# Four projection steps in a round: output products of a linear-attention mixer moved from the stage after it into its rounds

## Chip, cores, metric

The program runs on one core of one Trainium2 chip. The metric is the device time of one execution in microseconds; the time before is 2855.52 us, the median of three runs (2850.24 to 2856.83). Engines are named as the profile names them: PE (TensorE), DVE (VectorE), ACT (ScalarE), POOL (GpSimd) and SP, whose queue issues most DMAs.

## The reference, cut to what matters

One step of a two-layer trunk of width 1024 over 1072 columns (16 meta tokens, 32 frames of a running stream, 1024 of a new one). In layer 0 two mixers share one projection in and one out; mixer A is sliding-window attention, mixer B gated linear attention with four heads:

```python
def gla_chunk(S, q, k, v, g):
    b = jnp.cumsum(g, axis=2)
    decay = jnp.exp(jnp.where(causal[:, :, None], b[:, :, :, None, :] - b[:, :, None, :, :], -jnp.inf))
    att = jnp.einsum('bhtd,bhsd,bhtsd->bhts', q, k, decay)
    o = jnp.einsum('bhtd,bhdv->bhtv', q * jnp.exp(b), S) + jnp.einsum('bhts,bhsv->bhtv', att, v)
    bl = b[:, :, -1:, :]
    S_new = jnp.exp(bl[:, :, 0, :, None]) * S + jnp.einsum('bhsd,bhsv->bhdv', k * jnp.exp(bl - b), v)
    return S_new, o
...
gb = jax.nn.log_sigmoid((glr @ w_gate + b_gate)) / GATE_TAU           # the gate of mixer B
ob = rmsnorm(ob, onorm).reshape(B_, L, H_B * DV_B) * jax.nn.silu(rb)
x = x + jnp.concatenate([oa, ob], axis=-1) @ w_out                    # ab_output, both mixers
x = x + mlp(rmsnorm(x, norm_mlp[l]), w_up[l], w_down[l])              # each layer
```

Layer 1 (another mixer and its MLP) is not touched.

## The kernel before, in words

Activations lie transposed: 128 features on the partitions, tokens in the free dimension. `xT` (128 x 8 x 1072) is the residual. Every product in 32-bit accuracy is made of three matmuls: each operand is split into a high part (ACT, a cast, L64) and a low part (DVE, the difference, L66), and `mm3` adds high x high, high x low and low x high (L75, L76, L77).

`mixer_b` works through the nine token tiles (48 and eight of 128) in twelve rounds, t = -2 to 9, as a pipeline: a round makes the output of tile t-1 (`gla_output`: masked scores times values, states, norm and gate into `gl_sq`), the features of t+2 (transposes), the scores of t in six levels (`gla_levels`, two halves of three; `copy_predicated` on DVE writes them into `gl_att`, L662), the decays of t+1 (`gla_decays`: sums of gates by matmul, exponentials `gl_X` on ACT, and with them `gl_Q` and a new `gl_X` on DVE and POOL), the gate of t+2 (`gla_gate`), the inputs of t+1, the states of t (`gla_states`, `gl_S`, L685), and the transposes of the finished tile t-1 (`gla_finish`, L722) with the split into `mixb`. The gate log sigmoid(x) is min(x, 0) - ln(1 + exp(-|x|)): ACT makes the second part, DVE (L566) joins the two and reads x from PSUM.

The output projection fills PE between these parts. Its steps come from the generator `out_ab`, one at each `next(fill)`. A step is one product (`add_product`): 12 matmuls (four blocks of 128 features by three) into one PSUM bank, which DVE then adds into `xT` (L833). `ob` is one of eight blocks of 128 output features and has a weight tile of its own (`weights`: a DMA of 256 KB on SP's queue, then the split into `op_h` and `op_l`). Mixer A's part comes first, 8 x 3 = 24 products over `CHUNKS` (304, 384 and 384 columns); then mixer B's for the first of four `QUARTERS` (268 columns each) and ob 0 to 3, four products after the last round. The rounds take two steps each.

What is left of mixer B's part, 28 products, follows in `body`, here called the norm stage: quarter by quarter, `product(q, ob)`, its weights kept in `wb`. After a quarter, `spill(q)` stores it to DRAM (one DMA, on SP's queue), and `mlp_norm(q, between)` makes the sums of squares (`nm_acc`), PE's mean, the scaling of `xT` in place (L873) and the MLP's operands `ho_B`; `between` holds three products of the next quarter, issued between the squares and the mean. The MLP's first two products need quarters 0 and 1, its third (`ho_T`) the differences of all four.

PE's order in `mixer_b` is the order of the code (`manual_schedule`). The other engines' order, and PE's outside, is set by the framework's scheduler. All banks of one product, of transposes, decays, gate and states come in turn from one pool of four (`bank`): a request takes the buffer of the fourth request before it and waits for that buffer's last reader. The masked scores and the output have another pool of two (`b2`).

Of the kernel before, what the change touches and what calls it, by code (L numbers as in the profile page):

```python
# [12 lines left out]
AF = mybir.ActivationFunctionType  # L13
ALU = mybir.AluOpType
# [6 lines left out]
KB = 8  # L21
# [7 lines left out]
QUARTERS = [[(268 * q, 268 * q + 268) for q in range(4)], [(16 + 264 * q, 280 + 264 * q) for q in range(4)]]  # L29
# [22 lines left out]
class Core:  # L52
# [501 lines left out]
    def gla_gate(self, t, d, sb):  # L554
        nc = self.nc
        r0, m = TILES[t]
        px = self.bank()
        nc.tensor.matmul(px[:m, :256], self.aug[t % 2][:, :m], self.wg, start=True, stop=True)

        e = sb.tile([P, 256], F32, name="gl_e", bufs=1)  # L560
        g = sb.tile([P, 256], F32, name="gl_g", bufs=1)
        gh, gl = d["g"] = [sb.tile([P, 256], F32R, name=f"gl_g{x}") for x in "hl"]
        nc.scalar.activation(e[:m], px[:m, :256], AF.Abs)
        nc.scalar.activation(e[:m], e[:m], AF.Exp, scale=-1.0)
        nc.scalar.activation(e[:m], e[:m], AF.Ln, bias=1.0)
        nc.vector.scalar_tensor_tensor(g[:m], px[:m, :256], 0.0, e[:m], op0=ALU.min, op1=ALU.subtract)  # L566
        self.hi_lo(g[:m], gh[:m], gl[:m])


# [181 lines left out]
                pass  # L751


    ahead = 4

    def out_ab(self, sb, xs):
        w = self.i["w_out_ab"][0]
        for ob in range(KB):
            for k in (0, 1) if ob == 0 else (ob + 1,) if ob + 1 < KB else ():

                self.nc.vector.tensor_copy(self.xT[0:1, k, 0:1], self.z0[0:1, 0:1])
                self.nc.sync.dma_start(self.xT[:, k], xs[:, k])
            wt = self.weights(sb, w, 0, 4, P * ob, P, "op", 2)
            for c in CHUNKS:
                self.add_product(wt, self.mixa, 0, c, ob, c[0])
                yield
        for ob in range(self.ahead):
            wt = self.weights(sb, w, 4, 4, P * ob, P, "op", 2)
            self.add_product(wt, self.mixb, 0, QUARTERS[0][0], ob, 0)
            yield  # L770


    def mixer_b(self, fill):
        tc, nc = self.tc, self.nc
        with ExitStack() as st:
            self.b2 = st.enter_context(tc.tile_pool(name="myb2", bufs=2, space=PSUM, reuse_waits="tile"))
            sb = st.enter_context(tc.tile_pool(name="my2", bufs=2, reuse_waits="tile"))
            st.enter_context(tc.manual_schedule(engines={mybir.EngineType.PE}))
            n = len(TILES)
            d = {}  # L780

            def stage(f, t, *a):
                if 0 <= t < n:
                    f(t, d[t], *a)

            def load(t, what):
                if 0 <= t < n:
                    self.gla_load(t, d.setdefault(t, {}), sb, what)

            self.glq = [sb.tile([P, 2, 6, 2, 64], F32, name=f"gl_Q{x}", bufs=1) for x in range(2)]  # L790
            for q in self.glq:
                nc.gpsimd.memset(q, 0.0)
            load(0, "z")
            self.z0 = d[0]["z"]
            for t in range(-2, n + 1):
                load(t + 3, "z")
                load(t + 2, "r")
                load(t + 1, "v")
                stage(self.gla_output, t - 1, sb)
                stage(self.gla_features, t + 2, sb)  # L800
                next(fill)
                stage(self.gla_levels, t, (0, 1, 2))
                stage(self.gla_decays, t + 1, sb)
                stage(self.gla_gate, t + 2, sb)
                stage(self.gla_inputs, t + 1, sb)
                stage(self.gla_levels, t, (3, 4, 5))
                stage(self.gla_finish, t - 1)
                stage(self.gla_states, t, sb)
                next(fill)

            for _ in fill:
                pass

# [809 lines left out]
def body(tc, i, o):  # L1623
    C = Core(tc, i, o)
    nc = tc.nc
    with ExitStack() as st:
# [18 lines left out]
        def right(name):  # L1645
            return tc.tile_pool(name=name, bufs=1, side="right", reuse_waits="tile")

        C.bank = banks(st.enter_context(tc.tile_pool(name="bank", bufs=4, space=PSUM, reuse_waits="tile")))
        with right("h0") as h0:
            C.hp = [h0] * 3  # L1650
            mixes = ExitStack()
            with right("kv") as c1, right("w0") as wsb:
                fill = C.project_a(xs, wsb, c1)
# [11 lines left out]
        with mixes:  # L1665
            mix = mixes.enter_context(tc.tile_pool(name="mixb", bufs=1, reuse_waits="tile"))
            C.mixb = [mix.tile([P, 4, T], F32R, name=f"mixb_{x}") for x in "hl"]
            xp = st.enter_context(right("x1"))
            C.xT = xp.tile([P, KB, T], F32, name="xT")
            op = mixes.enter_context(tc.tile_pool(name="op", bufs=2, reuse_waits="tile"))  # L1670
            C.mixer_b(C.out_ab(op, xs))
            hpool = ExitStack()
            C.nm = mixes.enter_context(tc.tile_pool(name="nm1", bufs=1, reuse_waits="tile"))
            wb = {}
            with tc.tile_pool(name="op2", bufs=6, reuse_waits="tile") as op2:
                def weights(ob):
                    if ob not in wb:
                        raw = op.tile([P, 4, P], F32, name="op_", bufs=2)
                        sb = op if ob in (2, 3) else op2
                        wb[ob] = [sb.tile([P, 4, P], F32R, name=f"op_{x}", bufs=2 if sb is op else 6) for x in "hl"]  # L1680
                        nc.sync.dma_start(raw, i["w_out_ab"][0].rearrange("(k p) n -> p k n", p=P)[:, 4:8, P * ob:P * ob + P])
                        C.hi_lo(raw, *wb[ob])
                    return wb[ob]
                def product(q, ob):
                    c = QUARTERS[0][q]
                    C.add_product(weights(ob), C.mixb, 0, c, ob, c[0])

                C.mlp_begin(0)
                steps = [[partial(product, q, ob) for ob in range(0 if q else C.ahead, KB)] for q in range(4)]
                for q in range(4):  # L1690
                    while steps[q]:
                        steps[q].pop(0)()
                    C.spill(q)
                    if q < 3:
                        C.mlp_norm(q, [steps[q + 1].pop(0) for _ in range(3)])

        hpool, nms = ExitStack(), ExitStack()
        nxt, sq, ys = [], {}, {}
# [142 lines left out]
```

## Time and profile before

| | us |
|---|---|
| median of three runs | 2855.52 (2850.24 to 2856.83) |
| profiled execution, its own time | 2860.78 |
| its span | 2859.0 |
| mean granted clock of PE | 0.962 of full speed |
| mixer B (360 to 557.4) | 197.4 |
| norm stage (557.4 to 650.8, from the split of the last transposes to PE's start on `ho_T`) | 93.4 |

Times in the profile count from the span's start. In a table by stage each engine has its busy time and, in brackets, its instructions; behind them stand the clock that the throttle granted PE (1.00 is full speed), the share of the DMA engines' time and the data rate. A timeline row holds start, duration, engine, line, operation, output and inputs, shapes and count; in square brackets stands how long the engine had been idle and for whom. A row of waits holds total, number and longest.

### The profile page before, as it was taken

How to read it: one execution, taken by the hardware profiler on the slowest of the kernel's cores; microseconds unless marked ns; L12 is line 12 of the kernel's file. 1: busy time of each engine (PE TensorE's matmuls, PEld its weight loads, DVE VectorE, ACT ScalarE, POOL GpSimd, SP SyncE). 2: the span in 40 equal slices, each digit the busy share in tenths (PEclk: the TensorE clock that was granted, in tenths of full speed). 3: DMA queues.
4: the chain of work that ended last, by engine and by line, in shares of the span. 5: the costliest groups of instructions: out<-in, count | busy, mean ns of one | idle time of the engine just before them, and what ended most of it. 6: DMA issues, size and time to landing. Idle time of an engine off the chain costs nothing. (4 is left out here: it accounts for less than half of the span.)

```text
span 2859.0 us, 49166 instructions
## 1 busy us (share of the span) xinstructions
PE 2642.7 (92%) x18377; PEld 2452.5 (86%) x18391; DVE 1891.1 (66%) x3846; ACT 1265.2 (44%) x2820; POOL 631.0 (22%) x693
## 2 busy tenths in 40 slices
PE   5899988878999999999999978999977999999998
PEld 5888966768999999999789856788767999989998
DVE  5934376687676677578643556778788676677553
ACT  4435454243333335445333346666653333435342
POOL 3423354200000210003110244555521000111000
PEclk9999988999999999999999979999988999999999
DMA  6343241132544577544465374344322434486643
GB/s 192 101 133 103 73 140 43 31 112 92 163 131 153 208 231 218 171 136 121 119 197 168 116 175 128 88 100 103 77 85 71 157 135 156 173 265 204 198 141 102
DMA packets 355926, 393.77 MB, mean 138 GB/s; under 512 B 41503, under 2 KB 292088, under 8 KB 353640
## 3 DMA queue, kind: packets, MB, share of 16 engines
q1 hardware_dynamic: 338728, 305.50, 37.6%
q0 software_dynamic: 16960, 85.13, 8.2%
q8 instruction: 145, 2.38, 0.4%
q14 instruction: 93, 0.76, 0.1%
HBM read 263.94 MB, written 125.48 MB: 136 GB/s over the span
## 5 line engine op out<-in xcount | busy, mean ns | idle before, releaser
L75 PE MATMUL bank<-pj_wh,h 128*128 128x384 f32 (+3 forms) x832 | 298.0, 360 | 9.5 <-ACT pj_wh L64 7.0
L77 PE MATMUL bank<-pj_wh,h 128*128 128x384 f32 (+3 forms) x832 | 296.1, 357 | 6.1 <-DVE h L66 4.8
L76 PE MATMUL bank<-pj_wl,h 128*128 128x384 f32 (+3 forms) x832 | 296.4, 357 | 3.4 <-DVE pj_wl L66 3.4
L76 PE MATMUL mu_y<-md_u,md_w 128*128 128x268 f32 (+1 forms) x896 | 260.6, 291 | 12.4 <-DVE md_u L66 10.4
L77 PE MATMUL mu_y<-md_u,md_w 128*128 128x268 f32 (+1 forms) x896 | 260.1, 290 | 6.1 <-POOL md_w L68 6.1
L75 PE MATMUL mu_y<-md_u,md_w 128*128 128x268 f32 (+1 forms) x896 | 261.3, 292 | 1.1 <-ACT md_u L64 1.0
L75 PE MATMUL bank<-md_u,md_w 128*128 128x268 f32 (+1 forms) x896 | 257.4, 287 | 0.1
L76 PE MATMUL bank<-md_u,md_w 128*128 128x268 f32 (+1 forms) x896 | 255.9, 286 | 1.5 <-DVE md_u L66 1.5
L77 PE MATMUL bank<-md_u,md_w 128*128 128x268 f32 (+1 forms) x896 | 255.5, 285 | 0.0
L64 ACT CAST md_u<-md_ur 128x536 fp32r<-128x536 f32 (+1 forms) x224 | 141.5, 636 | 230.4 <-PE mu_y L77 110.8
L66 DVE TENSOR_TENSOR md_u<-md_ur,md_u 128x536 fp32r<-128x536 f32 (+1 forms) x220 | 155.7, 711 | 129.9 <-ACT md_u L64 129.8
L76 PE MATMUL mu_y<-ho_T,mu_w 128*128 128x268 f32 (+1 forms) x768 | 219.2, 285 | 0.8 <-DVE ho_T L66 0.8
L77 PE MATMUL mu_y<-ho_T,mu_w 128*128 128x268 f32 (+1 forms) x768 | 219.3, 286 | 0.0
L75 PE MATMUL mu_y<-ho_T,mu_w 128*128 128x268 f32 (+1 forms) x768 | 218.5, 285 | 0.0
L1298 POOL TENSOR_TENSOR fx_p<-fx_p,sm_den 128x144 f32<-128x144 f32 (+7 forms) x128 | 150.6, 1177 | 181.8 <-DVE sm_den L1297 165.0
L66 DVE TENSOR_TENSOR mu_w<-mu_raw,mu_w 128x512 fp32r<-128x512 f32 x160 | 110.0, 688 | 116.3 <-ACT mu_w L64 116.3
L76 PEld LDWEIGHTS mu_y<-md_u,md_w 128*128 128x128 f32 x896 | 172.9, 193 | 14.5 <-DVE md_u L66 12.1
L64 ACT CAST mu_w<-mu_raw 128x512 fp32r<-128x512 f32 x160 | 99.2, 622 | 188.0 <-PE bank L77 124.6
L77 PEld LDWEIGHTS mu_y<-md_u,md_w 128*128 128x128 f32 x896 | 173.0, 193 | 6.5 <-POOL md_w L68 6.5
L75 PEld LDWEIGHTS bank<-pj_wh,h 128*128 128x128 f32 x832 | 158.8, 191 | 22.2 <-ACT pj_wh L64 7.5
L75 PEld LDWEIGHTS mu_y<-md_u,md_w 128*128 128x128 f32 x896 | 173.2, 193 | 1.8 <-ACT md_u L64 1.8
L77 PEld LDWEIGHTS bank<-pj_wh,h 128*128 128x128 f32 x832 | 158.4, 190 | 17.6 <-DVE h L66 5.1
(544 smaller groups left out, 8168.3 us busy)
## 6 DMA issues: line engine op xcount, KB each, us to landing
md_raw<-in_w_down SPq DMA_DIRECT2D x160, 256.0 KB
mu_raw<-in_w_up SPq DMA_DIRECT2D x64, 512.0 KB
ud<-xT POOLq DMA_DIRECT2D x16, 1876.0 KB, 7.5
md_ur<-ud SPq DMA_DIRECT2D x112, 268.0 KB
ud<-xT POOLq DMA_DIRECT2D x16, 1848.0 KB, 10.1
md_ur<-ud SPq DMA_DIRECT2D x112, 264.0 KB
fh_ka<-zk SPq DMA_DIRECT2D x32, 260.0 KB
md_k<-in_w_down SPq DMA_DIRECT2D x8, 1024.0 KB
```

What stands on the lines that cost most here:

```text
L64: nc.scalar.copy(hi, src)
L66: nc.vector.tensor_tensor(lo, src, hi.bitcast(F32), op=ALU.subtract)
L75: mm(out, ah, bh, start=start, stop=False)
L76: mm(out, ah, bl, start=False, stop=False)
L77: mm(out, al, bh, start=False, stop=stop)
L1298: nc.gpsimd.tensor_tensor(p[:, :n], p[:, :n], den[:, 0:1].to_broadcast([P, n]), op=ALU.mult)
```

## The change

Rounds t = -2 to 5 take three steps of the projection and rounds 6 to 9 four, 40 in all. One stands at the round's start, ahead of the output; one between the inputs and the second half of the levels; one behind the states; and from t = 6 on, one behind the features. `out_ab` yields mixer A's 24 products and then 16 of mixer B, quarters 0 and 1 for all eight blocks; from t = 6 on the columns of both quarters are finished. The transposes come last in the round. In the norm stage 16 products remain (quarters 2 and 3); quarters 0 and 1 are spilled at its start, and the norms of quarters 0 and 1 each take three products of quarter 2 between their parts, that of quarter 2 three of quarter 3. The gate is read from PSUM by ACT alone: a Relu of -x gives -min(x, 0), and DVE's instruction works on the two results in SBUF.

```diff
@@ gla_gate
         nc.scalar.activation(e[:m], px[:m, :256], AF.Abs)
+        nc.scalar.activation(g[:m], px[:m, :256], AF.Relu, scale=-1.0)
         nc.scalar.activation(e[:m], e[:m], AF.Exp, scale=-1.0)
         nc.scalar.activation(e[:m], e[:m], AF.Ln, bias=1.0)
-        nc.vector.scalar_tensor_tensor(g[:m], px[:m, :256], 0.0, e[:m], op0=ALU.min, op1=ALU.subtract)
+        nc.vector.scalar_tensor_tensor(g[:m], e[:m], -1.0, g[:m], op0=ALU.mult, op1=ALU.subtract)
@@ out_ab
-        for ob in range(self.ahead):
+        for ob in range(KB):
             wt = self.weights(sb, w, 4, 4, P * ob, P, "op", 2)
-            self.add_product(wt, self.mixb, 0, QUARTERS[0][0], ob, 0)
-            yield
+            for c in QUARTERS[0][:2]:
+                self.add_product(wt, self.mixb, 0, c, ob, c[0])
+                yield
@@ mixer_b
+                next(fill)
                 stage(self.gla_output, t - 1, sb)
                 stage(self.gla_features, t + 2, sb)
-                next(fill)
+                if t > 5:
+                    next(fill)
                 stage(self.gla_levels, t, (0, 1, 2))
                 stage(self.gla_decays, t + 1, sb)
                 stage(self.gla_gate, t + 2, sb)
                 stage(self.gla_inputs, t + 1, sb)
+                next(fill)
                 stage(self.gla_levels, t, (3, 4, 5))
-                stage(self.gla_finish, t - 1)
                 stage(self.gla_states, t, sb)
                 next(fill)
+                stage(self.gla_finish, t - 1)
@@ body
-                steps = [[partial(product, q, ob) for ob in range(0 if q else C.ahead, KB)] for q in range(4)]
+                steps = [[partial(product, q, ob) for ob in range(KB)] for q in (2, 3)]
                 for q in range(4):
-                    while steps[q]:
-                        steps[q].pop(0)()
+                    left = steps[q - 2] if q > 1 else ()
+                    while left:
+                        left.pop(0)()
                     C.spill(q)
                     if q < 3:
-                        C.mlp_norm(q, [steps[q + 1].pop(0) for _ in range(3)])
+                        C.mlp_norm(q, [steps[q // 2].pop(0) for _ in range(3)])
```

PE in the second half of a full round before: the end of the decays (L608), the gate (L558), the second half of the levels (L656), the transposes (L722), the states in two chunks (L679), the product, and the output of the next round (L701). `bank_` and `b2_` with a number are PSUM requests, one number each; of a product its first matmul is shown.

```order
L608 MATMUL bank_4986<-gl_gh_4794,gl_end_1732 128x256
...
L558 MATMUL bank_4992<-gl_wg_1751,gl_aug0_1754 128x256
L656 MATMUL b2_5022<-gl_Q0_3920,gl_X_4744 128x128 x6
L722 MATMUL bank_5032<-ident_61,gl_sq_4887 128x128 x4
L679 MATMUL bank_5039<-gl_v_4678,gl_kd_4787 64x128 x4
L679 MATMUL bank_5047<-gl_v_4678,gl_kd_4787 64x128 x4
L75 MATMUL bank_5055<-mixa_h_1766,op_h_4917 128x384
...
L701 MATMUL b2_5076<-gl_v_4678,gl_att_4806 128x128
```

The same place after, with every line two higher for the levels, the states and the rest:

```order
L610 MATMUL bank_5092<-gl_gh_4885,gl_end_1732 128x256
...
L558 MATMUL bank_5098<-gl_wg_1751,gl_aug0_1754 128x256
L75 MATMUL bank_5129<-mixa_h_1766,op_h_4983 128x384
...
L658 MATMUL b2_5143<-gl_Q0_3920,gl_X_4835 128x128 x6
L681 MATMUL bank_5153<-gl_v_4761,gl_kd_4878 64x128 x4
L681 MATMUL bank_5161<-gl_v_4761,gl_kd_4878 64x128 x4
L75 MATMUL bank_5169<-mixa_h_1766,op_h_4983 128x384
...
L724 MATMUL bank_5183<-ident_61,gl_sq_5015 128x128 x4
L75 MATMUL bank_5203<-mixa_h_1766,op_h_5198 128x304
```

A product stands between the gate and the levels, the transposes behind the second product, and the third one ahead of the next output. Counted in requests of the pool of four, the product behind the states took the gate's buffer before (four requests on), and takes it still; the transposes take the buffer of the product behind the gate, and the round's opening product that of the first chunk of the states (L681, first row), which DVE frees in L685 (L687 after).

DVE at the start of the norm stage before, from the split of the last transposes (`mixb_l`) on: `op_l` are splits of weights, L833 the adds of products, L136 the sums of squares.

```order
L66 TENSOR_TENSOR mixb_l<-bank,mixb_h 128x4x128
L833 TENSOR_TENSOR xT<-xT,bank 128x384
L66 TENSOR_TENSOR op_l<-op__5830,op_h 128x512
L833 TENSOR_TENSOR xT<-xT,bank 128x268
...
L136 TENSOR_TENSOR nm_acc_5986<-nm_acc_5986,nm_t 128x268
...
L152 SCALAR_TENSOR_TENSOR nm_y<-nm_a,nm_y 128x268
L66 TENSOR_TENSOR op_l<-op__6090,op_h 128x512
L873 SCALAR_TENSOR_TENSOR xT<-xT,gain,nm_y 128x268 x8
```

DVE at the same place after:

```order
L66 TENSOR_TENSOR mixb_l<-bank,mixb_h 128x4x128
L136 TENSOR_TENSOR nm_acc_6107<-nm_acc_6107,nm_t 128x268 x2
L66 TENSOR_TENSOR op_l<-op__6130,op_h 128x512
L66 TENSOR_TENSOR op_l<-op__6150,op_h 128x512
...
L66 TENSOR_TENSOR op_l<-op__6275,op_h 128x512
...
L152 SCALAR_TENSOR_TENSOR nm_y<-nm_a,nm_y 128x268
...
L878 SCALAR_TENSOR_TENSOR xT<-xT,gain,nm_y 128x268 x8
```

The first quarter's sums of squares now stand right behind the split, and six weight splits (6130 to 6275) stand ahead of the first scaling, where eleven stood.

SP's queue at the end of mixer B and in the norm stage before: L818 are the weights in `out_ab`, L1681 those in `body`, L865 the spills, L903 the MLP's weights.

```order
L818 DMA op__5870<-in_w_out_ab 128x4x128
L1681 DMA op__5905<-in_w_out_ab 128x4x128
...
L1681 DMA op__6049<-in_w_out_ab 128x4x128
L865 DMA xsave_5904<-xT 1024x1x268
L1681 DMA op__6090<-in_w_out_ab 128x4x128
L865 DMA xsave_5904<-xT 1024x1x268 x2
L903 DMA mu_raw<-in_w_up 128x8x128 x4
```

The queue after:

```order
L823 DMA op__6050<-in_w_out_ab 128x4x128
L1686 DMA op__6130<-in_w_out_ab 128x4x128
L1686 DMA op__6150<-in_w_out_ab 128x4x128
L870 DMA xsave_6105<-xT 1024x1x268 x2
L1686 DMA op__6170<-in_w_out_ab 128x4x128
...
L1686 DMA op__6336<-in_w_out_ab 128x4x128
L870 DMA xsave_6105<-xT 1024x1x268
L908 DMA mu_raw<-in_w_up 128x8x128 x4
```

Two spills stand ahead of six of the eight weight loads, where one stood ahead of the last of eleven tiles.

More of the change, by code (lines that the diff above doesn't have):

```diff
@@ L751, in mixer_a @@
                 pass
-    ahead = 4
     def out_ab(self, sb, xs):
```

## The prediction

> **What bounds the kernel now.** I read the shares of the page first, then busy time by stage, then TensorE's waits in the two stages that the diff touches, and last the timelines of one round and of one product.
>
> ```profile
> PE 2642.7 (92%) x18377; PEld 2452.5 (86%) x18391; DVE 1891.1 (66%) x3846; ACT 1265.2 (44%) x2820; POOL 631.0 (22%) x693
> core 0: us, PE busy (x) PEld busy (x) DVE busy (x) ACT busy (x) POOL busy (x), PEclk, DMA share, GB/s
> 360.00:391.90 31.90, 23.39 (x146) 19.16 (x146) 23.59 (x65) 20.51 (x52) 20.37 (x32) 0.94 0.67 235
> 391.90:533.00 141.10, 118.40 (x748) 97.69 (x749) 99.21 (x269) 60.81 (x154) 62.99 (x97) 0.83 0.14 39
> 477.10:495.10 18.00, 14.19 (x111) 11.73 (x109) 14.43 (x40) 8.08 (x21) 8.21 (x13) 1.00 0.11 30
> 495.10:516.40 21.30, 18.59 (x109) 15.76 (x110) 13.22 (x37) 9.21 (x24) 8.67 (x14) 0.79 0.05 13
> 533.00:557.40 24.40, 21.16 (x137) 17.23 (x138) 11.34 (x34) 3.84 (x11) 0.75 (x1) 0.86 0.06 17
> 557.40:584.80 27.40, 21.02 (x147) 18.95 (x146) 15.82 (x32) 11.72 (x25) 1.80 (x2) 1.00 0.43 127
> 584.80:650.80 66.00, 44.49 (x317) 42.97 (x315) 59.14 (x108) 29.10 (x51) 5.92 (x6) 0.84 0.34 98
> ```
>
> Over the whole span TensorE is the bound (92%), but not in these two stages. Mixer B runs from 360 to 557.4: the opening, seven full rounds (391.9 to 533, 20.16 us each), and the end. The norm stage runs from 557.4 to 650.8; there VectorE is busy for 15.82 + 59.14 = 75.0 of 93.4 us and TensorE for 65.5. What TensorE waits for, first in mixer B, then in the norm stage:
>
> ```profile
> PE bank L75 <- DVE gl_g L566: 12.7, 5, 3.0
> PE b L701 <- DVE gl_att L662: 8.0, 3, 3.5
> PE bank L722 <- DVE gl_sq L712: 6.8, 3, 4.3
> PE bank L75 <- ACT ho_T L64: 12.1, 1, 12.1
> PE bank L75 <- ACT op_h L64: 5.5, 5, 3.2
> ```
>
> The largest wait of mixer B is a product that may not enter its PSUM bank before VectorE has read the gate out of it (L566); the next two are the masked scores and the scaled output, also VectorE's. In the norm stage TensorE idles 12.1 us for the operand of the MLP's third product, the end of VectorE's chain of norms and differences. One round shows the order:
>
> ```profile
> 477.12 0.38 PE L701 MATMUL b<-gl_v,gl_att 128*128 128x128 f32 x2
> 480.62 0.42 PE L75 MATMUL bank<-mixa_h,op_h 128*128 128x384 f32 x1
> 482.80 1.50 PE L656 MATMUL b<-gl_Q,gl_X 128*128 128x128 f32 x12
> 485.77 0.28 PE L608 MATMUL bank<-gl_gh,gl_end 128*128 128x256 f32 x1
> 492.03 0.41 PE L75 MATMUL bank<-mixa_h,op_h 128*128 128x304 f32 x1 [2.66 <-DVE gl_g L566]
> 495.14 0.38 PE L701 MATMUL b<-gl_v,gl_att 128*128 128x128 f32 x1 [1.19 <-DVE gl_att L662]
> 513.17 0.45 PE L75 MATMUL bank<-mixa_h,op_h 128*128 128x384 f32 x1 [2.66 <-DVE gl_g L566]
> 515.46 0.52 PE L75 MATMUL bank<-mixa_h,op_h 128*128 128x384 f32 x1
> 515.78 0.52 PE L76 MATMUL bank<-mixa_l,op_h 128*128 128x384 f32 x1
> 606.04 0.29 PE L75 MATMUL bank<-mixb_h,op_h 128*128 128x268 f32 x1
> 609.01 0.28 PE L75 MATMUL bank<-mixb_h,op_h 128*128 128x268 f32 x1
> ```
>
> A 384-column product of mixer A takes 482.80 - 480.62 = 2.18 us at full clock (12 matmuls, 0.18 each). After the wait at 513.17 the pitch is 0.32: half the clock, and the round that begins at 495.1 runs at 0.79 for it. So a wait is paid twice. A product of 268 columns takes 12 of the 24 steps between the last two rows, 1.49 us. By columns a 304 one takes 1.73, and the mean over mixer A's three sizes is 2.03.
>
> **Term 1, the full rounds.** Each gets a third product; once mixer A's 24 are used up (eight rounds), four of 268 columns, 5.95 us against 6.1, so I count them alike. TensorE's own work in the warm round is 18.00 - 2.66 - 1.19 = 14.15; with the third product 16.2. VectorE gets one more add: 14.43 + 0.5 = 14.9. Neither fills 18 us, so the round's length hangs on the chain that frees the bank of its opening product. In the new order that is the bank from which VectorE took the states' update (L685) in the round just ended:
>
> ```profile
> 485.65 1.11 DVE L712 SCALAR_TENSOR_TENSOR gl_sq<-b,gl_y,gl_rs 128x128 f32<-128x128 f32 x4
> 486.68 0.81 DVE L600 TENSOR_TENSOR gl_Q<-gl_X,gl_qkT 64x128 f32<-64x128 f32 x2
> 491.90 0.59 DVE L685 SCALAR_TENSOR_TENSOR gl_S<-gl_S,gl_bl,bank 128x128 f32<-128x128 f32 x2
> 486.82 0.39 ACT L563 ACTIVATE gl_e<-bank 128x256 f32<-128x256 f32 x1
> ```
>
> Product 2.18, output to decays 485.77 - 477.12 - 2.18 = 6.47, then 0.91 until VectorE's features start (486.68), then 5.22 until the states' update (491.90) and 0.59 for it: 15.4. To this come the work that VectorE may take in ahead of it, one more add (0.5) and the scaled output (L712, 1.11; it stands before the features now and may come behind them): 17.0. I take 17.5 warm, a little above the chain. The round of 20.16 holds 2.16 of half clock over the warm 18.0; with the gate's wait (2.66 a round) gone or under 1 us I keep half, 1.1. That makes 18.6 a round and 7 x -1.56 = **-11**. Ends: all of the half clock stays, 19.66, -3.5; none stays and the chain alone binds, 17.4, -19.
>
> At this place the clock decides, and the row at 513.17 shows a fall after a wait of 2.66 us. The Trainium skill (TensorE: Matmul & The Clock Gate, section "Why this matters for your kernels") asks for no idle gaps over about 3 us between bursts and gives half rate as the price. The price agrees with the pitches 0.32 and 0.18; the threshold doesn't, as the 2.66 shows. By that rule waits cut to a third would leave the clock full and the sum would take the end at -19; that is rival A below.
>
> **Term 2, opening and end.** The opening (31.9 us) takes twelve products for eight, 4 x 2.03 = 8.1 more. It has idle TensorE time of 31.9 - 23.39 = 8.5, which can cover most; VectorE and GpSimd (23.59 and 20.37) aren't full there. I take +3 (0 to +6). The end (24.4 us) has eight products of 268 (11.9) for two of mixer A and four of 268 (about 10): +1.9, while its idle TensorE time of 24.40 - 21.16 = 3.2 mostly goes, and a clock of 0.86 rises. I take -1.5 (-3 to +2).
>
> **Edits at nothing.** The gate's second reading by ScalarE (nine times 0.39) lies beside a ScalarE busy for 8.08 of 18 us; it lengthens the way to the gate by 0.39, which the next round alone needs. Four more weight tiles are loaded and split in the rounds, where the DMA share is 0.14. Moving the transposes (L722) behind the last product takes them off the wait for gl_sq (6.8 in all) and makes the copy into mixer B's operand later; only products that come five rounds on, and in the last round the norm stage, read it. If VectorE had no spare time in the rounds this cover would be gone; it has 3.1 us a round.
>
> **Term 3, the norm stage.** Of its 28 products of mixer B, 12 are in the rounds now and 16 stay. The rows of VectorE:
>
> ```profile
> 557.43 0.69 DVE L66 TENSOR_TENSOR mixb_l<-bank,mixb_h 128x512 fp32r<-128x512 f32 x1 [1.04 <-ACT mixb_h L64]
> L833 DVE TENSOR_TENSOR xT<-xT,bank 128x268 f32<-128x268 f32 (+1 forms) x33 | 14.0, 432 | 8.6 <-PE bank L77 8.4
> L66 DVE TENSOR_TENSOR op_l<-op__6090,op_h 128x512 fp32r<-128x512 f32 x1 | 0.7, 694 | 1.3 <-ACT op_h L64 1.3
> DVE op_l L66 <- ACT op_h L64: 8.0, 8, 1.5
> 574.72 0.37 SPq L1681 DMA_DIRECT2D op__6049<-in_w_out_ab  x1
> 577.95 0.63 ACT L64 CAST op_h<-op__6049 128x512 fp32r<-128x512 f32 x1 [0.77 <-DMA op__6049<-in_w_out_ab]
> 577.61 0.37 SPq L1681 DMA_DIRECT2D op__6090<-in_w_out_ab  x1
> 583.58 0.62 ACT L64 CAST op_h<-op__6090 128x512 fp32r<-128x512 f32 x1 [1.51 <-DMA op__6090<-in_w_out_ab]
> 648.34 0.59 PE L75 MATMUL bank<-ho_T,mu_w 128*128 128x268 f32 x1 [12.06 <-ACT ho_T L64]
> ```
>
> VectorE's work falls by 17 adds at 0.43 (33 to 16) and three splits at 0.69 (the row of op_l is one of eleven alike; eight stay): 75.0 - 7.3 - 2.1 = 65.6. Its idle time is 93.4 - 75.0 = 18.4 now, nearly all of it waits for products (8.4) and for weights (8.0). With half the products 8.4 becomes about 4; eight weights of eleven make 8.0 into 5.8. Against that, two spills now stand ahead of six weight loads on SP's queue, and one spill ahead made the load of 577.61 take 5.97 us to its cast instead of 3.23, +2.7. The scaling of the first quarter, which stood behind eleven splits on VectorE, stands behind six. I take 9 us of idle: 74.6, which is **-18.8**. Ends: no idle -27.8; all 18.4 stay -9.4.
>
> **Sum.** -11 + 3 - 1.5 - 18.8 = -28.3. The profiled execution took 2860.8, so 2832.5 in its terms; it lies 5.3 above the median of the runs (2855.5), which puts the median after at **2827.2**. All good ends together: -19 + 0 - 3 - 27.8 = -49.8, 2805.7; all bad ones: -3.5 + 6 + 2 - 9.4 = -4.9, 2850.6.
>
> **Rivals.** A, the clock holds: with waits under 1 us the half-clock stretches go altogether: -19 + 3 - 1.5 - 18.8 = -36.3, **2819.2**. For it: they stand right behind waits. Against: the chain (17.0) is longer than TensorE's work (16.2), so some wait per round is left. Chance 0.15.
>
> B, the waits come back under other names: the opening product waits for the states' update, or the output's first matmul for the masked scores (L662, 3.5 us at longest now), and rounds stay at 20.16. Sum +3 - 1.5 - 18.8 = -17.3, **2838.2**. For it: VectorE ends the round today too (the 1.19 at 495.14). Chance 0.17.
>
> C, the norm stage keeps its idle time, since norms are a chain and the weights come late behind the spills: -11 + 1.5 - 9.4 = -18.9, **2836.6**. For it: the 2.7 us of one spill. Chance 0.12.
>
> D, slower: TensorE has no room in the rounds, and the 16 added products cost their full time there: 4 x 2.03 + 12 x 1.49 = 26.0 warm with every wait kept, while the norm stage gives 18.8 back: +7.2, **2862.7**. It decides as soon as more than 18.8 of these 26.0 us are not covered. Against: TensorE idles 22.7 us in the full rounds (141.1 - 118.4), and the longest wait goes by the edit. Chance 0.05.
>
> **Chances.** The forecast 0.51, A 0.15, B 0.17, C 0.12, D 0.05. About 0.2% (5.7 us) is what a measurement of this kernel can tell from no change. B and C together would give 2847, and D with a part of the gains falls near no change; so faster 0.89, same 0.06, slower 0.05. The range holds the forecast and A to C, with the ends of their terms: 2808 to 2847. What is left out: D, and A with all of the norm stage's idle time gone.
>
> **What would show it.** Right: rounds near 18.6 us with three products and no wait for the gate over 1 us, a granted clock there above 0.9, VectorE near 66 us busy from the last transposes to the third MLP operand, and that stretch near 75. Wrong in term 1: rounds of 20 us or more, with waits for gl_S, gl_att or xT of 2 us behind the products, and a clock of 0.83. Wrong in term 3: over 12 us of VectorE idle there, waiting for ScalarE's op_h, the weights behind the spills. The prediction falls if the added products lengthen the rounds by about their own 2 us.

## The result, and the profile after

The changed kernel took 2818.22 us (median; 2815.87 to 2824.49) against 2856.18 (2850.24 to 2862.49) for the kernel before: a ratio of 0.9869, interval 0.9854 to 0.9885, so 33 to 42 us faster. The forecast was 2827.2, in a range of 2808 to 2847; rival A, the clock that holds, stood at 2819.2. The profiled execution took 2817.04 (span 2815.3). Its span is 43.7 shorter than the one of before, more than the 38.0 between the medians, since the profiled execution of before lay 4.6 above its median and this one lies 1.2 below. The sums below are between these two traces.

The busy time by stage, with columns as before. The opening is the first row, the seven full rounds the second, then two single rounds, the end, and the norm stage in two pieces:

```profile
core 0: us, PE busy (x) PEld busy (x) DVE busy (x) ACT busy (x) POOL busy (x), PEclk, DMA share, GB/s
359.60:389.90 30.30, 28.91 (x195) 25.28 (x193) 24.50 (x70) 21.53 (x56) 20.74 (x31) 1.00 0.75 257
389.90:510.60 120.70, 114.86 (x857) 96.23 (x856) 104.39 (x280) 64.24 (x164) 65.89 (x98) 1.00 0.20 55
457.50:474.80 17.30, 16.65 (x122) 14.07 (x122) 15.40 (x41) 9.95 (x26) 9.69 (x15) 1.00 0.20 59
474.80:492.10 17.30, 16.51 (x133) 14.06 (x134) 14.58 (x41) 9.86 (x26) 8.19 (x14) 1.00 0.17 47
510.60:533.10 22.50, 21.78 (x182) 18.55 (x180) 14.51 (x42) 4.52 (x13) 0.75 (x1) 1.00 0.19 58
533.10:560.50 27.40, 20.80 (x124) 18.84 (x125) 23.33 (x47) 17.05 (x40) 5.36 (x6) 0.88 0.42 126
560.50:607.70 47.20, 22.47 (x140) 20.91 (x139) 43.31 (x73) 20.81 (x33) 12.93 (x2) 0.76 0.40 114
```

The rounds take 17.24 us instead of 20.16, with three or four products instead of two, and the granted clock is 1.00 where it was 0.83. The norm stage takes 74.6 instead of 93.4. TensorE's waits from 392 to 530 (total, number, longest), and from its timeline the openings of three rounds and the matmul that ends the norm stage:

```profile
PE bank L75 <- DVE gl_S L687: 4.1, 7, 0.8
PE b L703 <- DVE gl_att L664: 0.6, 1, 0.6
PE bank L724 <- DVE xT L838: 0.4, 1, 0.4
```

```profile
457.54 0.38 PE L75 MATMUL bank<-mixa_h,op_h 128*128 128x304 f32 x1 [0.61 <-DVE gl_S L687]
474.78 0.36 PE L75 MATMUL bank<-mixb_h,op_h 128*128 128x268 f32 x1 [0.60 <-DVE gl_S L687]
492.12 0.36 PE L75 MATMUL bank<-mixb_h,op_h 128*128 128x268 f32 x1 [0.82 <-DVE gl_S L687]
607.70 0.59 PE L76 MATMUL bank<-ho_T,mu_w 128*128 128x268 f32 x1 [1.90 <-DVE ho_T L66]
```

The waits for the gate (12.7), the masked scores (8.0) and the scaled output (6.8) are gone, but for 0.6; what is left is 0.6 to 0.8 us a round, at the product that opens it, for the states' update. In the norm stage, VectorE's waits, and its adds as a group:

```profile
DVE op_l L66 <- ACT op_h L64: 2.8, 2, 1.8
DVE nm_a L151 <- ACT nm_a L150: 2.8, 1, 2.8
DVE xT L838 <- PE bank L77: 0.3, 1, 0.3
```

```profile
L838 DVE TENSOR_TENSOR xT<-xT,bank 128x268 f32<-128x268 f32 x16 | 6.7, 423 | 0.4 <-PE bank L77 0.3
```

VectorE is busy for 66.6 of 74.6 us. Its waits for products (8.4 before) shrank to 0.3, those for weights from 8.0 to 2.8, and one of 2.8 for a norm is new. By stages the 43.7 us are: opening -1.6 (31.9 to 30.3), rounds -20.4, end -1.9 (24.4 to 22.5), norm stage -18.8, everything else -1.0.

### The profile page after: what moved, and what is told of

Same layout as the page of the kernel before. It is cut to its first block, busy times and chain, and to the rows that moved or that the text cites. A ratio compares the mean times of both kernels' runs of the same rounds, so it can differ in the third digit from the quotient of the medians.

```text
span 2815.3 us, 49213 instructions
## 1 busy us (share of the span) xinstructions
PE 2624.8 (93%) x18391; PEld 2437.4 (87%) x18391; DVE 1892.2 (67%) x3850; ACT 1266.0 (45%) x2833; POOL 634.5 (23%) x693
## 4 chain that ended last, share of the span: by engine, by line
PE 75%; DVE 11%; DMA 4%; ACT 2%; issue 2%; POOL 1%; SPq 0%; DVEq 0%; ACTq 0%; POOLq 0%
PE bank L75 12%; PE bank L76 12%; PE bank L77 12%; PE mu_y L76 8%; PE mu_y L77 8%; PE mu_y L75 8%; PE bank L1490 3%; PE bank L1500 2%; PE bank L1501 1%; DMA md_ur<-ud 1%; PE fx_s L1472 1%; PE fx_s L1473 1%; PE bank L257 1%; DMA md_raw<-in_w_down 1%; DVE xT L878 1%
## 5 line engine op out<-in xcount | busy, mean ns | idle before, releaser
L76 PEld LDWEIGHTS mu_y<-md_u,md_w 128*128 128x128 f32 x896 | 172.4, 192 | 15.2 <-DVE md_u L66 12.8
L77 PEld LDWEIGHTS mu_y<-md_u,md_w 128*128 128x128 f32 x896 | 172.3, 192 | 6.5 <-POOL md_w L68 6.5
L76 PEld LDWEIGHTS bank<-pj_wl,h 128*128 128x128 f32 x832 | 160.3, 193 | 15.9 <-DVE pj_wl L66 4.4
```

The costliest lines, as they stand in the source:

```text
L76: mm(out, ah, bl, start=False, stop=False)
L77: mm(out, al, bh, start=False, stop=stop)
```

## The experiments

Each has its edit, the expectation as written ahead of it, and the medians; "against before" is the ratio to the kernel before on the same chip, with its interval. The groups of experiments ran on different chips, where the kernel before took 2854.1 to 2856.2 us.

**e1_gate_psum: the changed kernel with the gate of before.**

```diff
-        nc.scalar.activation(g[:m], px[:m, :256], AF.Relu, scale=-1.0)
-        nc.vector.scalar_tensor_tensor(g[:m], e[:m], -1.0, g[:m], op0=ALU.mult, op1=ALU.subtract)
+        nc.vector.scalar_tensor_tensor(g[:m], px[:m, :256], 0.0, e[:m], op0=ALU.min, op1=ALU.subtract)
```

> The changed kernel with the gate as before: VectorE joins min(x, 0) and the logarithm and reads x from PSUM. Theory (the gate's early reading is needed for the short rounds): the product behind the states (at 489.08 in the round from 474.8) must wait for VectorE's gate, which stood at 490.52 to 491.1 there, so a wait of about 2 us for gl_g returns in each full round, and with it stretches of half clock; rounds of 18.7 (the wait alone) to 20.2 us instead of 17.25, +10 to +21 us, about 2835. Rival (the third product alone hides the wait, since it stands between the gate and the next use of its bank): no wait for gl_g over 0.6 us, 2818 within 3.

Measured: 2812.36 us, 0.9851 against before (0.983 to 0.9872). The theory fell. The rival's mechanism holds, since no wait for the gate returns, but the kernel is not the same: its rounds are shorter. Openings of two rounds on TensorE:

```profile
454.24 0.38 PE L75 MATMUL bank<-mixa_h,op_h 128*128 128x304 f32 x1 [0.18 <-DVE gl_S L686]
470.71 0.36 PE L75 MATMUL bank<-mixb_h,op_h 128*128 128x268 f32 x1 [0.18 <-DVE gl_S L686]
```

VectorE's gate (L567) and the small instruction L89 behind it, grouped from 392 to 510:

```profile
L567 DVE SCALAR_TENSOR_TENSOR gl_g<-bank,gl_e 128x256 f32<-128x256 f32 x6 | 2.4, 408 | 0.0
L89 DVE SCALAR_TENSOR_TENSOR gl_y<-gl_a,gl_y 128x4 f32<-128x4 f32 x6 | 1.5, 242 | 0.0
```

The same groups in the changed kernel:

```profile
L568 DVE SCALAR_TENSOR_TENSOR gl_g<-gl_e,gl_g 128x256 f32<-128x256 f32 x6 | 4.0, 665 | 0.0
L89 DVE SCALAR_TENSOR_TENSOR gl_y<-gl_a,gl_y 128x4 f32<-128x4 f32 x6 | 3.2, 525 | 0.0
```

A round is 16.47 us instead of 17.24. Reading the gate from two tiles in SBUF instead of PSUM and SBUF costs VectorE 0.26 us, and the next instruction another 0.28, on the average of six; in the round that ends at 474.78 they took 0.74 and 0.71 against 0.41 and 0.29 here, which is nearly the whole difference of 0.77. Both lie ahead of the states' update, so the opening product waits for them. No wait for the gate returns: a product now stands between the gate and the next use of its bank, where the shorter transposes stood before.

**e9_relu_psum: is it the operands or the added ScalarE instruction?** Here ScalarE still makes the Relu, but writes it to PSUM. e12_changed_again is the changed kernel once more, on the same chip.

```diff
-        nc.scalar.activation(g[:m], px[:m, :256], AF.Relu, scale=-1.0)
+        nc.scalar.activation(px[:m, :256], px[:m, :256], AF.Relu, scale=-1.0)
-        nc.vector.scalar_tensor_tensor(g[:m], e[:m], -1.0, g[:m], op0=ALU.mult, op1=ALU.subtract)
+        nc.vector.scalar_tensor_tensor(g[:m], e[:m], -1.0, px[:m, :256], op0=ALU.mult, op1=ALU.subtract)
```

> The changed kernel, but ScalarE writes its Relu back into the gate's PSUM bank, and VectorE reads one operand from PSUM and one from SBUF, as in e1_gate_psum. Theory (VectorE's gate instruction, and L89 behind it, take longer in the change because with both operands in SBUF they meet GpSimd, 0.74 and 0.71 us against 0.41 and 0.29): rounds of 16.5, as e1_gate_psum, 2812. Rival (the additional ScalarE instruction delays the gate): rounds of 17.25, 2818.

> The changed kernel once more, beside e9_relu_psum on the same chip: 2818 within 3, so that e9_relu_psum differs from it by 5 to 7 us (theory) or by less than 2 (rival).

Measured: 2817.87 (2810.63 to 2821.72) and 2822.64 (2813.09 to 2825.70). The difference of 4.8 is just under the expected 5 to 7, and both lie some 5 above what was expected for them; the runs of the two overlap, so the times alone don't settle it. The traces do for the rounds: e9's open 16.47 us apart, as in e1, e12's 17.24. Two openings of e9, and its gate as a group:

```profile
442.07 0.38 PE L75 MATMUL bank<-mixa_h,op_h 128*128 128x304 f32 x1 [0.18 <-DVE gl_S L687]
458.54 0.38 PE L75 MATMUL bank<-mixa_h,op_h 128*128 128x304 f32 x1 [0.18 <-DVE gl_S L687]
```

```profile
L568 DVE SCALAR_TENSOR_TENSOR gl_g<-gl_e,bank 128x256 f32<-128x256 f32 x6 | 2.4, 406 | 0.0
```

So it is the operands, and not the added ScalarE instruction. The Trainium skill (SBUF — State Buffer, section "SBUF: two separate sides") says that a VectorE instruction with two SBUF inputs and a GpSimd instruction that reads SBUF exclude one another. 406 against 665 ns on the average, with GpSimd at work on `gl_Q` and `gl_X` beside it, agrees; single ones took from 0.41 to 0.75 us in the changed kernel.

**e2_gate_only: the kernel before with the gate edit alone.** The edit is the reverse of e1's.

> The kernel before with the gate edit alone (ScalarE reads x by Abs and by Relu, VectorE works in SBUF). Theory (one wait of a round stands in front of another): the wait of 2.66 us for the gate goes, but the next round's output still needs VectorE's last masked scores (gl_att), which end at 495.1 either way; the idle time moves in front of the output, rounds stay at 19 to 20 us, 0 to -8 us against before. Rival (the gate's wait and the half clock it causes are the whole loss of the rounds): rounds of 17.3 to 18, -15 to -20 us.

Measured: 2866.23, ratio 1.0039 (1.0026 to 1.0051): slower by about 11 us. The theory was right that the idle time moves in front of the output, and wrong on what that gives: it expected 0 to -8 us, with rounds of 19 to 20, and they take 21.6. Waits and the busy time from 392 to 530:

```profile
PE b L702 <- DVE gl_att L663: 24.1, 6, 4.7
```

```profile
392.00:530.00 138.00, 113.90 (x679) 92.46 (x679) 88.23 (x241) 58.82 (x153) 57.42 (x85) 0.80 0.14 40
```

Two waits a round became one of 2.5 to 4.7 us in front of the output, and the clock fell from 0.83 to 0.80.

**e3_finish_old: the transposes back ahead of the states.**

```diff
+                stage(self.gla_finish, t - 1)
                 stage(self.gla_states, t, sb)
                 next(fill)
-                stage(self.gla_finish, t - 1)
```

> The changed kernel with the transposes back ahead of the states. Theory (the bank ring counts): the product behind the states then takes the bank of the product behind the gate, which VectorE adds only at 490.2 to 490.6 (wait of 0.5 to 1.5 us), and the states come 0.6 us later; rounds 0.5 to 2 us longer, +4 to +14 us, about 2826. Rival (the place of the transposes is nothing, as gl_sq was ready at 487.4, ahead of the end of the levels at 488.5): 2818 within 3.

Measured: 2834.93, 0.9924 (0.9907 to 0.9941), some 17 slower than the change. The place of the transposes counts, but in the main not for the bank that the theory named:

```profile
PE bank L724 <- DVE gl_sq L714: 12.2, 5, 2.5
PE bank L75 <- DVE xT L838: 2.7, 2, 1.7
```

```profile
392.00:530.00 138.00, 121.61 (x842) 102.36 (x842) 103.01 (x275) 64.31 (x163) 65.88 (x98) 0.93 0.17 48
```

The rows are waits and busy time from 392 to 530. In the rounds with three products the transposes wait up to 2.5 us for the scaled output, and a round takes 20.6 (the first 21.4). In the last two of the seven, with four products, that wait is gone (17.3 and 19.2 us); there the product behind the states waits 1.1 and 1.7 us for `xT`, which is the theory's wait.

**e4_open_late: the opening product behind the output.**

```diff
-                next(fill)
                 stage(self.gla_output, t - 1, sb)
+                next(fill)
```

> The changed kernel with the opening product of each round moved behind the output. Theory (the opening product covers the wait for the masked scores): the output's first matmul waits for gl_att, which ended at 476.3 where TensorE was free at 474.2, about 2 us in each full round, and the clock falls in some; +8 to +20 us, about 2832. Rival (the round is bound by the chain of states, bank and opening product, and without that product at its head it falls to TensorE's own 16.6 us): -4 us.

Measured: 2856.97, 1.0006 (0.9994 to 1.0017): the whole gain is gone, by one line. The norm stage stays short (72.7), the seven rounds grow to 159.9. The waits from 392 to 530, two outputs in the timeline, and the busy time in two pieces of one round, behind the wait and later:

```profile
PE b L703 <- DVE gl_att L664: 17.8, 6, 3.1
```

```profile
451.94 0.79 PE L703 MATMUL b<-gl_v,gl_att 128*128 128x128 f32 x2 [3.06 <-DVE gl_att L664]
475.82 0.79 PE L703 MATMUL b<-gl_v,gl_att 128*128 128x128 f32 x2 [3.06 <-DVE gl_att L664]
```

```profile
452.00:462.00 10.00, 10.00 (x43) 7.66 (x44) 3.46 (x8) 2.67 (x9) 0.72 (x1) 0.50 0.24 73
462.00:475.00 13.00, 10.76 (x80) 9.56 (x78) 11.96 (x33) 6.48 (x17) 8.91 (x14) 1.00 0.12 29
```

One wait of 3.06 us per round is followed by 10 us at a clock of 0.50, in which VectorE is busy for 3.46 only: it now waits for TensorE, and the round gets to 23.9.

**e10_late_filled: e4 with more work in front of its wait.** Each set of transposes is made five times, with the same result.

```diff
-        for h in range(4):
+        for h in 5 * (0, 1, 2, 3):
             nc.tensor.transpose(pt[:, h, :m], sq[:m, P * h:P * h + P], self.ident[:m, :m])
```

> e4_open_late with each set of transposes made five times (the same result again): about 2.1 us more work for TensorE in each round, in front of the place where it waits 3.07 us for gl_att. Theory (a wait of 3 us costs itself and some 4 us of half clock behind it): the wait falls under 1 us, the clock stays full, rounds of 23.9 become 18.5 to 19.5, -30 us against e4_open_late, about 2826. Rival (the rounds of e4_open_late are long by their dependences, and the half clock only fills the wait): no gain, 2857 or up to 15 us more.

Measured: 2836.59, 0.9936 (0.9924 to 0.9949), 20 us faster than e4 with more work for TensorE. Two outputs and the rounds between:

```profile
454.21 0.49 PE L703 MATMUL b<-gl_v,gl_att 128*128 128x128 f32 x2 [0.69 <-DVE gl_att L664]
473.05 0.49 PE L703 MATMUL b<-gl_v,gl_att 128*128 128x128 f32 x2 [0.69 <-DVE gl_att L664]
```

```profile
454.20:491.90 37.70, 36.33 (x275) 31.49 (x275) 31.95 (x82) 20.05 (x51) 18.53 (x28) 1.00 0.16 46
```

A round falls from 23.88 to 18.84. The forecast of -30 was too high: the output at 412.17 still waits 1.40, with 10 us of half clock behind it, and that round takes 23.2. Two shorter waits were followed by half clock as well, which the matmuls behind the first show (304 columns, 0.25 apart; 0.14 at full clock):

```profile
392.29 0.39 PE L703 MATMUL b<-gl_v,gl_att 128*48 128x128 f32 x2 [0.79 <-DVE gl_att L664]
395.60 0.46 PE L76 MATMUL bank<-mixa_l,op_h 128*128 128x304 f32 x1
395.85 0.46 PE L77 MATMUL bank<-mixa_h,op_l 128*128 128x304 f32 x1
511.38 0.49 PE L703 MATMUL b<-gl_v,gl_att 128*128 128x128 f32 x2 [1.27 <-DVE gl_att L664]
```

**e11_before_filled: the same test on the kernel before**, whose state matmuls are made four times.

```diff
-            for h in range(4):
+            for h in 4 * (0, 1, 2, 3):
                 rows = slice(64 * (h % 2), 64 * (h % 2) + 64)
                 nc.tensor.matmul(pd[rows, h // 2], kd[a:a + w, 64 * h:64 * h + 64], v[a:a + w, P * h:P * h + P], start=True, stop=True)
```

> The kernel before with each chunk's state matmuls made four times (start each time anew, the same result): about 2 us more work for TensorE in each round, in front of the wait for the gate (2.66). Theory (the half clock behind the waits costs the kernel before about 2 us a round): waits under 1 us, a full clock, rounds of 20.2 become 18 to 18.5, -10 to -15 us, about 2843. Rival: no gain, 2855 or more.

Measured: 2834.64, 0.9937 (0.9923 to 0.9950), 19.5 us faster than before, by work that nobody needs, and more than the 10 to 15 expected. Waits and busy time from 392 to 530:

```profile
PE b L701 <- DVE gl_att L662: 2.8, 4, 1.0
PE b L656 <- DVE gl_att L662: 1.5, 1, 1.5
PE bank L75 <- DVE gl_g L566: 0.4, 1, 0.4
```

```profile
392.00:530.00 138.00, 133.00 (x1243) 113.85 (x1242) 107.79 (x291) 64.14 (x160) 63.69 (x98) 1.00 0.16 44
```

The seven rounds (392.04 to 512.62) have no wait over 1 us, the one of 1.5 lies behind them, the clock is full, and they take 120.6 us: within 0.2 of the changed kernel's 120.7, while two products a round and the norm stage (91.4) are those of before. The 64 state matmuls of a round take 3.34 us where 16 took 0.68. So the rounds of before had at least 2.7 us of TensorE time each for the taking, and the change fills it with products instead.

**e8_order_only: the changed places, but two steps a round.** Before's `ahead`, gate and norm stage.

```diff
+                next(fill)
                 stage(self.gla_output, t - 1, sb)
                 stage(self.gla_features, t + 2, sb)
-                next(fill)
...
-                stage(self.gla_finish, t - 1)
                 stage(self.gla_states, t, sb)
                 next(fill)
+                stage(self.gla_finish, t - 1)
```

> The kernel before with its gate, its 24 + 4 steps and its norm stage, but two steps of a round in the changed places: one opens the round, one stands behind the states, and the transposes come last. Theory (order makes the round, the number of steps fills it): the same chain through VectorE of 16.5 to 17 us, but TensorE has only 14.2 us of work, so 2 to 3 us of wait per round remain and the clock falls in most; rounds of 18 to 20, -5 to -15 us, about 2845. Rival (order alone is the whole gain of the rounds): rounds of 16.5 to 17.2 and a full clock, -22 us, about 2833.

Measured: 2851.09, 0.9988 (0.9976 to 0.9999). Waits and busy time from 392 to 530:

```profile
PE bank L722 <- DVE gl_sq L712: 21.4, 5, 5.5
```

```profile
392.00:530.00 138.00, 109.54 (x750) 91.37 (x749) 98.82 (x272) 58.64 (x151) 61.81 (x94) 0.89 0.14 37
```

The rival is refuted: order without the third product leaves TensorE idle in front of the transposes instead, and a round takes 19.8, within the theory's 18 to 20. The gain, some 3.5 us, is less than the theory's 5 to 15.

**e5_split_only: the split of the change without its rounds.** Sixteen products are drained behind the last round of the kernel before, and 16 are left in the norm stage.

```diff
-        for ob in range(self.ahead):
+        for ob in range(KB):
             wt = self.weights(sb, w, 4, 4, P * ob, P, "op", 2)
-            self.add_product(wt, self.mixb, 0, QUARTERS[0][0], ob, 0)
-            yield
+            for c in QUARTERS[0][:2]:
+                self.add_product(wt, self.mixb, 0, c, ob, c[0])
+                yield
...
```

> The kernel before with its rounds and gate, but with the 16 products of quarters 0 and 1 drained behind the last round (and 16, not 28, in the norm stage). Theory (moving products away from the norm stage gains only if the rounds cover them): the end of mixer B grows by twelve products of 1.49 us, 17.9, the norm stage shrinks by about 18.8; 2854 within 5. Rival (the norm stage's gain stands by itself, since TensorE is not its bound): about 2837.

Measured: 2856.49, 1.0002 (0.9989 to 1.0015): no gain, as the theory said. The drained products and what follows:

```profile
556.28:580.60 24.32, 24.32 (x196) 24.32 (x195) 14.29 (x28) 8.59 (x16) 1.52 (x2) 1.00 0.30 87
580.60:649.20 68.60, 42.43 (x268) 39.86 (x266) 62.65 (x116) 34.46 (x64) 7.52 (x6) 0.83 0.45 130
```

From the last transposes to the MLP's third operand it is 93 us, as before: 24.3 of them for the 16 drained products, without a gap. The 18.8 of the norm stage are won only where the rounds take the products for nothing.

**e6_spill_pool and e7_split_pool: what bounds the norm stage now.** Both start from e1_gate_psum, whose norm stage takes 74.6 as the change's. e6 puts two spills on GpSimd's queue, e7 makes eight weight splits there.

```diff
-        self.nc.sync.dma_start(self.xsave[:, :, c0:c1], self.xT[:, :, c0:c1])
+        (self.nc.gpsimd if self.l == 0 and q < 2 else self.nc.sync).dma_start(self.xsave[:, :, c0:c1], self.xT[:, :, c0:c1])
...
-                        C.hi_lo(raw, *wb[ob])
+                        C.hi_lo(raw, *wb[ob], "p")
```

> The changed kernel with the gate read from PSUM by VectorE (e1_gate_psum), and the first two spills on GpSimd's DMA queue, so that no weight load stands behind them on SP's. Theory (the norm stage is VectorE's, but about 7 us of its 74.6 are waits for weights and for the chain of norms): the waits for op_h (4.2 of VectorE, 3.1 and 0.5 of TensorE) shrink, the norm stage falls by 1 to 4 us; 2810. Rival (the weights' way is hidden behind the norms): same as e1_gate_psum, 2812 within 2.

> e1_gate_psum with the low parts of the norm stage's eight weight tiles made on GpSimd (8 x 0.69 us off VectorE). Theory (GpSimd is held up while VectorE works from SBUF: one of its adds of 128x268 took 12.0 us at 575 there, against 0.8): the splits come late, products wait for op_l, and the stage gets longer by 3 to 15 us; 2815 to 2828. Rival (VectorE's work is all that counts): -5.5 us, 2807.

Measured: 2812.18 (0.9851, 0.9837 to 0.9864) and 2809.86 (0.9846, 0.9833 to 0.9860): neither can be told from e1 by its time, which is what e6's rival expected. The norm stage of e6, then of e7, from the last transposes' split to the MLP's third operand, and one of e7's splits:

```profile
531.81:605.55 73.74, 43.73 (x261) 40.81 (x262) 66.30 (x119) 37.71 (x73) 15.26 (x9) 0.79 0.42 121
```

```profile
534.56:606.71 72.15, 44.71 (x262) 41.62 (x262) 65.72 (x111) 37.99 (x73) 18.71 (x16) 0.78 0.42 122
```

```profile
L68 POOL TENSOR_TENSOR op_l<-op__6141,op_h 128x512 fp32r<-128x512 f32 x1 | 1.5, 1466 | 0.0
```

The spills ahead of the weights cost the stage 0.9 us, not the 2.7 of a single load. e7's theory was wrong: GpSimd's splits took 1.3 to 1.5 us each and were not held up. It was VectorE's other work that grew beside them. Eight splits, 5.9 us in e1, were taken off VectorE, yet its busy time is only 0.5 us below e1's 66.2 and the stage 2.4 shorter: the sums of squares (L136) took 608 ns for 480, their last adds (L139) 700 for 431, the scalings (L877) 536 for 489, and with the splits of `ho_B` and `ho_T` this is 5.2 us. One of these adds, beside a GpSimd split of 1.50 us that began at 549.59:

```profile
549.87 1.52 DVE L139 TENSOR_TENSOR nm_acc<-nm_acc,nm_acc 128x268 f32<-128x268 f32 x1
```

The profiled execution of e7 was its slowest (2819.04), so the 2.4 of the stage rests on that one trace.

## Why the prediction was right, and which terms were off

The gain came where it was expected, but more of it: between the two traces -28.3 was forecast and -43.7 measured. The medians agree better, 2827.2 and 2818.2, for a reason that is luck: the trace of before was taken to lie 5.3 above its median, and that of the change lies 1.2 below. By the same luck rival A's 2819.2 meets the median to 1 us, while its -36.3 falls 7.4 short between the traces.

*Norm stage, -18.8 forecast, -18.8 measured.* VectorE was put at 65.6 us busy and 9 idle; it was 66.6 and 8.0. Inside the idle part the shares were off: waits for products 0.3 (4 expected), for weights 2.8 (5.8), and 2.8 for a norm that was not listed. That the sum is met to 0.1 is therefore luck in part: 1.0 too little for the work, 1.0 too much for the idle time. The prices (33 to 16 adds, three splits) held. The bound named, VectorE, fits its 66.6 busy of 74.6 us, but no run takes work off it cleanly (in e7 its other instructions grew). e5 shows the condition that the term rested on.

*Full rounds, -11 forecast, -20.4 measured.* The failing step is "I keep half, 1.1" of the half clock: none was left. The chain, 17.0 and taken as 17.5, was 17.24 with its wait of 0.6. So 1.1 of the 1.36 us a round that were missed are the clock, the rest the margin on the chain. The term's good end (-19) was passed by 1.4, since it took 17.4 for the chain alone; the 17.0 of its own sum would give -22. That 17.24 lies so near 17.0 is luck in part. The sum has an opening product of 384 columns (2.18), but those that open the rounds have 304 (1.73) or 268, and it leaves out the gate's 0.77 (below). Less 0.45 it would be 16.55, and without the gate's edit the round takes 16.47 (e1). Rival A's condition, waits under 1 us, came true, and e11 and e10 show its mechanism by themselves: TensorE kept busy in front of a wait keeps its clock. The argument against A, that the chain leaves some wait, was true (0.6) and did not matter.

*Opening and end, +1.5 forecast together, -3.5 measured.* The opening's idle time covered four more products altogether: TensorE is busy for 28.91 of 30.30 us at full clock, and the stage got 1.6 shorter. The end was put at -1.5 and is -1.9.

*The gate, at nothing.* This was wrong: only ScalarE's second instruction was priced, and not that VectorE's instruction changed from one operand in PSUM to two in SBUF. e1 and e9 put it at 0.77 us a round, 4.6 us over the seven rounds. The longest wait, the gate's, went by the new places of the products and not by the edit: without the edit (e1) it stays away, and with the edit alone (e2) the kernel is slower. Whether the third product is needed for it is not shown: in e8, without one, no wait for the gate is left either, since there the transposes take its bank, and wait longer for `gl_sq`.

*The other edits.* The transposes' place was held to cost nothing and to end a wait; e3 prices it at 17 us. Rival D, added products paid in full, did not come true. e5 comes nearest to it, with twelve products more behind the rounds, and comes out at no change.

*On the clock.* The Trainium skill (TensorE: Matmul & The Clock Gate, section "Why this matters for your kernels") puts the price at half rate, which the clock of 0.50 in e4's row agrees with, and the limit near 3 us of idle time. The forecast set that limit aside for the 2.66 us at 513.17; e3's waits of 2.5 us with a clock of 0.93 speak the same way. But the forecast laid the 0.79 of the round from 495.1 to that one wait, and most of it lies earlier:

```profile
492.00:496.50 4.50, 3.28 (x22) 2.62 (x24) 3.39 (x9) 1.04 (x2) 3.24 (x3) 1.00 0.00 0
497.00:503.00 6.00, 6.00 (x26) 4.96 (x26) 0.96 (x2) 3.33 (x9) 0.00 (x0) 0.50 0.16 44
```

Behind the wait of 2.66 that ended at 492.03 the clock stayed full for 4.5 us, and 6 us at half clock came behind a second one of 1.19 (495.14). So the length of one wait does not decide. In the changed kernel waits of up to 0.8 us a round left the clock at 1.00, and so did the 1.5 in e11; in e10 half clock followed some 2.5 us behind single waits of 0.79 and 1.27. Which pattern of idle time lowers the clock stays open. What e10 and e11 show is that more work in front of the waits brings the clock back: from 392 to 530 it was 0.94 in e10 (0.79 in e4) and 1.00 in e11 (0.83 before).

The version that does best by its parts is e1_gate_psum: the change without its gate edit, with rounds of 16.47 us of which TensorE is busy for all but 3%, as 112.92 of 116.10 us show:

```profile
390.30:506.40 116.10, 112.92 (x858) 96.09 (x857) 99.36 (x279) 63.47 (x158) 65.20 (x96) 1.00 0.21 57
```

Its interval overlaps that of the change, so by time alone it is not told apart. e6 and e7, which are built on it, came out at 2812 and 2810 us as well.

## What to carry to other kernels

In a loop that two engines share, look where TensorE waits each time round (2 to 3 us here), and put independent matmuls in front of just that wait: here they cost nothing, and they won back the half clock behind it too. The place decides: in e4 one product a place too late cost the whole gain. Repeating matmuls that are there already tells in one run how much is to be had, before any work is moved. When an operand moves from PSUM to SBUF to release a bank, count what the reading instruction then shares with GpSimd.

## What was not expected of the hardware

Useless matmuls made the kernel before 19.5 us faster (e11), and e4 20 us (e10). Moving one product by one place brought a wait of 3.06 us in most rounds, 10 us at half clock behind each, and cost 39 us in all (e4 against the change). In e10 a single wait of 0.79 us was followed by half clock. A VectorE instruction of 128x256 took 406 ns with one operand in PSUM and 665 with both in SBUF beside GpSimd, and one of 128x4 behind it 242 and 525.
